# One attention unit of a decoder trunk, laid out anew over all engine queues

## The chip, the cores and the metric

The kernel runs on one core of one Trainium2 chip. Its time is the device time of one execution, in microseconds (us). TensorE is called PE here and its weight loads PEld, VectorE is DVE, ScalarE is ACT, GpSimd is POOL, and SP is the engine whose queue issues most transfers. Each engine works through its own queue in program order, and waits there for what it needs from the others.

## The reference

The reference is one layer of a decoder trunk over 2048 positions of width 1024. One wide product gives queries, keys, values, gates and the input of a pooling branch; a sliding-window attention with sinks and a multi-scale causal pool are mixed through gates, projected, and normalised. What matters here is the attention: 16 query heads share 2 key heads, and each block of 128 queries sees 256 keys.

```python
logits = jnp.einsum('bnqhgd,bnkhd->bnhgqk', qb, kb) * (HEAD_DIM ** -0.5) + bias
logits = jnp.where(mask[None, :, None, None], logits, NEG_INF)
probs = jax.nn.softmax(jnp.concatenate([logits, sink], axis=-1), axis=-1)[..., :-1]
out = jnp.einsum('bnhgqk,bnkhd->bnqhgd', probs.astype(v.dtype), vb)
...
a = sliding_window_sink_attention(q, k, v, sinks[l], bias, mask) * jax.nn.silu(a_gate)
p = jnp.einsum('bsgc,gcd->bsgd', multiscale_causal_pool(p_in), w_pool_mix[l]).reshape(B, S, POOL_WIDTH)
```

## The kernel before

The kernel goes through five stages: gate products, attention over the first 1024 positions, gate products again, attention over the second 1024, and the projections with the normalisation. A product in full precision is made of rounded high parts and the rests (low parts): a function `low` subtracts the rounded high part from a number, and three matmuls replace one.

The function `attention` runs once for each half. It has 64 units, numbered `n`; a unit is two heads of one block of 128 queries. Its loop makes five turns more than that, in which the last units drain. A unit passes through a pipeline that spans several turns of the loop:

- PE makes its scores, `lg` (`score_mms`, four matmuls of 256 columns).
- For each of the two heads, DVE adds the bias to the scores and takes the running minimum of the negated sum (`tensor_tensor_reduce`, which the profile calls CUSTOM_DVE_ANT_0; writes `L` and `nm`), and ACT makes the exponentials of it in place, with their sum (`sm`).
- DVE takes the reciprocal of the two sums. ACT scales head 0 with it and DVE scales head 1 (`tensor_scalar`).
- PE turns the probabilities (`turn_mms`, into the bank `pt`), ACT rounds them to `pth`, and DVE makes the low part `ptl` from `pt` and `pth`.
- PE multiplies both with the values (`value_mms`, into the bank `pv`). High and low halves of the values lie in two halves of the partitions, so ACT copies one half to `o2`, and DVE adds it to the other, into `o` (two additions).

The buffers `pt`, `pv`, `pth` and `ptl` exist once, `lg` twice, `L` three times. Beside this, each turn of the loop holds a piece of other work: `project(n)` issues 9 or 12 matmuls of 512 columns from another product, which give later queries and the pooling input (`fill_one` issues 12 matmuls of the next stage in the last turns). When such a product ends, its result is taken at the end of a turn: `take_q` makes two ACT casts and two DVE operations that form new queries `qs`; `pool_sums` and `pool_diff` do the pooling on ACT, POOL and DVE (`vb`, `nxt`). Splitting weights into parts (`w_set`) uses ACT, and POOL or DVE.

No scheduler reorders these: the helper class `Ordered` keeps an engine's instructions in the order in which the Python code issues them, so all of them carry line 56 of that helper in the profile. The order of the statements in the loop is thus the order in each queue.

Of the kernel before, what the change touches and what calls it, by code (L numbers as in the profile page):

```python
# [59 lines left out]
def kernel(  # L60
# [675 lines left out]
    def attention(ph, s, q0, nxt):  # L736
# [149 lines left out]
        bts = {0: bias_tile(0)}  # L886
        raw_q = {}
        parts, accs, sums = {}, {}, {}
        lgs, exps, Ls, pvs, outs, ags, pgs = {}, {}, {}, {}, {}, {}, {}
        opened = []  # L890
        act.activation(warm, mhalf, AF.Exp)

# [32 lines left out]
        for n in range(N + 5):  # L925
# [1 line left out]
            if n == 0:  # L927
                project(n)
            if n < N:
                lgs[n] = score_mms(j, n % U, b, qs[j, t])  # L930
            pt = None
            if n - 2 in Ls:
                L, k0 = Ls.pop(n - 2)
                pt = turn_mms(L, k0)
            if n - 1 in exps:
                sm = exps[n - 1][2]
                dve.reciprocal(sm, sm)
            if n - 3 in pvs:
                pv = pvs.pop(n - 3)
# [5 lines left out]
                o2 = tp.tile([HD, 2, P], F32, tag="o2", bufs=2, name="o2")  # L945
                act.copy(o2, pv[HD:])
                for h in range(2):
                    dve.tensor_tensor(
                        outs[jj, tt][h * HD : (h + 1) * HD, bb * P : (bb + 1) * P], pv[0:HD, h, :], o2[:, h, :], ALU.add
                    )  # L950
            if n - 1 in exps:
                E, e0, sm = exps[n - 1]
                act.activation(E[:, 0, e0:256], E[:, 0, e0:256], AF.Copy, scale=sm[:, 0:1])
            if pt is not None:
                h0 = k0 // P
                pth = tp.tile([P, 2, 2, P], F32R, tag="pth", bufs=1, name="pth")
                ptl = tp.tile([P, 2, 2, P], F32R, tag="ptl", bufs=1, name="ptl")
                act.copy(pth[:, h0:], pt[:, h0:])
            if n < N:
                lg, c0 = lgs.pop(n)  # L960
                L = tp.tile([P, 2, 260], F32, tag="L", bufs=3, name="L")
                nm = tp.tile([P, 2], F32, tag="nm", bufs=4, name="nm")
                sm = tp.tile([P, 2], F32, tag="sm", bufs=4, name="sm")
                act.copy(L[:, :, 256], nsink[:, 2 * j : 2 * j + 2])
                for h in range(2):
                    dve.tensor_tensor_reduce(
                        L[:, h, c0:256],
                        lg[:, h, c0:],
                        bts[j][:, h, c0:],
                        1.0,  # L970
                        nsink[:, 2 * j + h : 2 * j + h + 1],
                        ALU.add,
                        ALU.min,
                        nm[:, h : h + 1],
                    )
                    act.activation(
                        L[:, h, c0:257],
                        L[:, h, c0:257],
                        AF.Exp,
                        bias=nm[:, h : h + 1],  # L980
                        scale=-1.0,
                        accum_out=sm[:, h : h + 1],
                    )
                exps[n] = (L, c0, sm)
# [10 lines left out]
            if pt is not None:  # L995
# [549 lines left out]
```

## Time and profile before

| | |
|---|---|
| median of 3 runs | 1771.92 us (1771.76 to 1773.22) |
| profiled execution | 1771.75 us, its span 1769.9 us, granted clock 0.992 |
| PE busy | 1701.8 us, 96% of the span |
| PEld busy | 1422.5 us, 80% |
| DVE, ACT, POOL busy | 68%, 53%, 45% |
| attention stages | about 424 to 690 us and 1030 to 1300 us from the start |

Busy time says how much of the span an engine had an instruction under way. The ends of matmuls are modelled in this profile and the rows overlap by some 0.15 us, so a PE row that follows at once begins before the modelled end of the one ahead. A row of the timeline gives start, length, engine, line, operation, written tile and read tiles, and in brackets how long the engine sat idle before it and what released it. Rows with "x4" are merged neighbours.

### The profile page before, as it was taken

Reading aid. Unit: us, or ns where it says so; the run is one execution under the profiler, and the core shown is the slowest. Engines: PE = TensorE matmul, PEld = TensorE weight load, DVE = VectorE, ACT = ScalarE, POOL = GpSimd, SP = SyncE. Lnnn points to the kernel's source line nnn. Section 1 sums busy time; section 2 is a strip of 40 time slices with the busy share of each in tenths; the row PEclk is TensorE's granted clock in tenths of the full one; section 3 lists DMA queues with packets and bytes.
Section 4 is the critical chain, followed back from the end, with each engine's and each line's share of the span. In section 5 each row is a group of like instructions: output and inputs, shape, how many; then the busy total and the mean of one; then the engine's idle time right before and its main releaser. Section 6 shows DMA issues by size and latency. Waiting matters only on the chain. (4 is left out here: it accounts for less than half of the span.)

```text
span 1769.9 us, 24992 instructions
## 1 busy us (share of the span) xinstructions
PE 1701.8 (96%) x8224; PEld 1422.5 (80%) x8224; DVE 1212.4 (68%) x2188; ACT 941.5 (53%) x1983; POOL 803.5 (45%) x624
## 2 busy tenths in 40 slices
PE   6899999999999998999999999999999989999997
PEld 5688888888888887888788888888878767888785
DVE  5977656546777777767745457777867676865777
ACT  4644444436777776444444367777744333423452
POOL 2155444530545567433424224455763663363542
PEclk9999999999999999999999999999999999999998
DMA  9385767853434467687776544454696684699432
GB/s 364 119 287 178 266 215 262 286 130 125 167 135 166 147 230 301 242 276 262 260 273 230 188 162 163 141 178 136 246 355 221 191 261 170 240 322 366 155 143 107
DMA packets 182161, 383.40 MB, mean 217 GB/s; under 512 B 18944, under 2 KB 39440, under 8 KB 182032
## 3 DMA queue, kind: packets, MB, share of 16 engines
q1 hardware_dynamic: 175392, 366.02, 59.1%
q0 software_dynamic: 3552, 11.56, 1.7%
q10 hardware_dynamic: 3088, 4.23, 0.9%
q8 instruction: 65, 1.06, 0.2%
q14 instruction: 64, 0.52, 0.1%
HBM read 245.40 MB, written 139.49 MB: 217 GB/s over the span
## 5 line engine op out<-in xcount | busy, mean ns | idle before, releaser
L56 PE MATMUL mm<-set_B,w_set 128*128 128x512 f32 x3096 | 768.5, 395 | 12.4 <-DVE w_set L133 5.5
L56 PEld LDWEIGHTS mm<-set_B,w_set 128*128 128x128 f32 x3096 | 577.3, 189 | 134.2 <-DVE w_set L133 10.6
L56 PE MATMUL lg<-set_T,w_set 128*128 128x512 f32 x2160 | 523.6, 392 | 17.3 <-DVE w_set L133 9.3
L56 PEld LDWEIGHTS lg<-set_T,w_set 128*128 128x128 f32 x2160 | 404.2, 188 | 110.8 <-DVE w_set L133 14.9
L133 DVE TENSOR_TENSOR w_set<-W,w_set 128x1024 fp32r<-128x1024 f32 x168 | 232.2, 1382 | 205.4 <-ACT w_set L326 195.2
L326 ACT CAST w_set<-W 128x1024 fp32r<-128x1024 f32 x168 | 176.3, 1050 | 266.8 <-PE mm L56 204.9
L56 PE MATMUL mm<-set_T,w_set 128*128 128x512 f32 x1032 | 257.6, 394 | 0.0
L56 PEld LDWEIGHTS mm<-set_T,w_set 128*128 128x128 f32 x1032 | 192.3, 189 | 39.5
L295 POOL TENSOR_TENSOR W<-W,A 128x512 f32<-128x512 f32 x58 | 86.5, 1491 | 237.9 <-DMA A<-in_win_dram 58.2
L304 POOL TENSOR_TENSOR W<-W 128x512 f32<-128x512 f32 x58 | 81.8, 1410 | 189.0 <-DVE w_set L133 178.7
L56 ACT ACTIVATE L<-L,nm 128x257 f32<-128x257 f32 (+1 forms) x256 | 127.1, 498 | 11.0 <-DVE nm L56 5.7
L299 POOL TENSOR_TENSOR W<-W 128x512 f32<-128x512 f32 x58 | 92.0, 1587 | 89.5 <-DVE w_set L133 80.4
L56 DVE TENSOR_TENSOR o<-pv,o 64x128 f32<-64x128 f32 x256 | 72.4, 283 | 81.0 <-ACT o L56 77.9
L56 DVE CUSTOM_DVE_ANT_0 L<-lg,bt,nsink 128x256 f32<-128x256 f32 (+1 forms) x256 | 111.6, 473 | 5.7 <-PE lg L56 1.7
L300 POOL TENSOR_TENSOR W<-W 128x512 f32<-128x512 f32 x58 | 94.6, 1630 | 43.8 <-DMA W<-in_win_dram 27.6
L56 POOL TENSOR_TENSOR p<-nxt,pg 128x512 f32<-128x512 f32 x32 | 41.3, 1292 | 113.5 <-DVE sm L56 113.0
L56 POOL TENSOR_TENSOR nxt<-vb 128x512 f32<-128x512 f32 (+3 forms) x32 | 34.2, 1068 | 122.7 <-ACT vb L56 122.7
L56 DVE TENSOR_TENSOR ptl<-pt,pth 128x512 fp32r<-128x512 f32 (+1 forms) x128 | 85.6, 669 | 1.7 <-ACT pth L56 1.5
L56 ACT COPY o<-pv 64x256 f32<-64x256 f32 x128 | 47.3, 370 | 66.1 <-PE pv L56 65.0
L56 DVE TENSOR_TENSOR k_lo<-spare,k_hi 128x512 fp32r<-128x512 f32 x61 | 61.4, 1009 | 30.0 <-ACT k_hi L56 13.2
L56 ACT ACTIVATE L<-L,sm 128x256 f32<-128x256 f32 (+1 forms) x128 | 64.3, 502 | 31.6 <-DVE sm L56 31.6
L56 PE MATMUL lg<-kk,qs 128*128 128x256 f32 (+1 forms) x512 | 80.3, 279 | 0.0
(217 smaller groups left out, 2347.3 us busy)
## 6 DMA issues: line engine op xcount, KB each, us to landing
W<-in_win_dram SPq DMA_DIRECT2D x48, 512.0 KB, 4.9
w_set<-wmix_d SPq DMA_DIRECT2D x28, 512.0 KB, 4.7
W<-in_win_dram SPq DMA_DIRECT2D x36, 256.0 KB, 3.2
A<-in_win_dram SPq DMA_DIRECT2D x36, 256.0 KB, 4.5
ag_d<-sig SPq DMA_DIRECT2D x32, 256.0 KB, 3.5
pg_d<-sig SPq DMA_DIRECT2D x32, 256.0 KB, 3.5
ma_d<-sig SPq DMA_DIRECT2D x32, 256.0 KB, 4.0
mp_d<-sig SPq DMA_DIRECT2D x32, 256.0 KB, 3.7
```

The costliest lines, as they stand in the source:

```text
L56: return lambda *args, **kw: self.tc.keep_in_program_order(op(*args, **kw))
L133: engine.tensor_tensor(dst, src, as32(hi), ALU.subtract)
L295: e.tensor_tensor(self.w[:, 1, :], self.w[:, 2, :], self.a22, ALU.add)
L299: e.tensor_tensor(x[:, 1, :], x[:, 1, :], x[:, 0, :], ALU.subtract)
L300: e.tensor_tensor(x[:, 2, :], x[:, 0, :], x[:, 2, :], ALU.subtract)
L304: e.tensor_tensor(x[:, 3, :], x[:, 3, :], x[:, 1, :], ALU.subtract)
L326: a.copy(by_two(hi), raw)
```

## The change

Nothing is computed differently, and no instruction is added or removed. The statements in the loop of `attention` stand in another order:

- the value products of a unit are issued one turn later, behind the next unit's scores and ahead of the turning of the unit between;
- the other work of the turn (`project` or `fill_one`) is issued straight after the PE work of the attention;
- ACT copies the sink column and scales head 0 ahead of the copy `o2` and the rounding to `pth`;
- the minimum and the exponentials are made for head 1 first, then head 0;
- on DVE the two additions into `o` come behind the two minima, ahead of the low part `ptl`;
- the reciprocal and the scaling of head 1 come at the end of the unit's own turn, behind its exponentials, and no longer in the next turn.

```diff
             if n < N:
-                lgs[n] = score_mms(j, n % U, b, qs[j, t])
-            pt = None
+                lg, c0 = score_mms(j, n % U, b, qs[j, t])
+            pt = pv = None
+            if n - 3 in turned:
+                pv = value_mms((n - 3) // U, (n - 3) % U, *turned.pop(n - 3))
             if n - 2 in Ls:
                 L, k0 = Ls.pop(n - 2)
-                pt = turn_mms(L, k0)
-            if n - 1 in exps:
-                sm = exps[n - 1][2]
-                dve.reciprocal(sm, sm)
-            if n - 3 in pvs:
...
+                pt, h0 = turn_mms(L, k0), k0 // P
+            if 0 < n < 60:
+                project(n)
+            elif n >= 60:
+                fill_one(n)
...
+                act.copy(L[:, :, 256], nsink[:, 2 * j : 2 * j + 2])
             if n - 1 in exps:
-                E, e0, sm = exps[n - 1]
-                act.activation(E[:, 0, e0:256], E[:, 0, e0:256], AF.Copy, scale=sm[:, 0:1])
+                E, e0, r = exps.pop(n - 1)
+                act.activation(E[:, 0, e0:256], E[:, 0, e0:256], AF.Copy, scale=r[:, 0:1])
+                Ls[n - 1] = (E, e0)
+            if pv is not None:
+                o2 = tp.tile([HD, 2, P], F32, tag="o2", bufs=2, name="o2")
+                act.copy(o2, pv[HD:])
             if pt is not None:
...
                 act.copy(pth[:, h0:], pt[:, h0:])
-                for h in range(2):
+            for h in (1, 0) if n < N else ():
                     dve.tensor_tensor_reduce(
...
+            if pv is not None:
...
                 for h in range(2):
                     dve.tensor_tensor(
                         outs[jj, tt][h * HD : (h + 1) * HD, bb * P : (bb + 1) * P], pv[0:HD, h, :], o2[:, h, :], ALU.add
                     )
             if pt is not None:
                 low(dve, ptl[:, h0:], pt[:, h0:], pth[:, h0:])
-            if n - 1 in exps:
-                E, e0, sm = exps.pop(n - 1)
-                dve.tensor_scalar(E[:, 1, e0:256], E[:, 1, e0:256], sm[:, 1:2], None, ALU.mult)
-                Ls[n - 1] = (E, e0)
-            if 0 < n < 60:
-                project(n)
-            elif n >= 60:
-                fill_one(n)
-            if pt is not None:
-                pvs[n - 2] = value_mms((n - 2) // U, (n - 2) % U, k0, pth, ptl)
+                turned[n - 2] = k0, pth, ptl
+            if n < N:
+                dve.reciprocal(sm, sm)
+                dve.tensor_scalar(L[:, 1, c0:256], L[:, 1, c0:256], sm[:, 1:2], None, ALU.mult)
+                exps[n] = (L, c0, sm)
```

How the queues stand is shown at one place, in the first attention: the turn whose end takes new queries, and the turn behind it. In these lists `mm<-set,w_set` are the matmuls of `project`, `pv` the value products, `lg` the scores, and `pt` the turning. First PE, before:

```order
L56 MATMUL mm<-set_B_68,w_set 128x512 x3
L56 MATMUL mm<-set_T_237,w_set 128x512 x6
L56 MATMUL pv<-pth,vv 128x256
L56 MATMUL pv<-ptl,vv 128x256
L56 MATMUL pv<-pth,vv 128x256
L56 MATMUL pv<-ptl,vv 128x256
L56 MATMUL lg<-kk,qs 128x256 x4
L56 MATMUL pt<-ident,L 128x128 x4
L56 MATMUL mm<-set_T_237,w_set 128x512 x6
```

and PE at the same place after the change:

```order
L56 MATMUL mm<-set_B_68,w_set 128x512 x3
L56 MATMUL mm<-set_T_237,w_set 128x512 x6
L56 MATMUL lg<-kk,qs 128x256 x4
L56 MATMUL pv<-pth,vv 128x256
L56 MATMUL pv<-ptl,vv 128x256
L56 MATMUL pv<-pth,vv 128x256
L56 MATMUL pv<-ptl,vv 128x256
L56 MATMUL pt<-ident,L 128x128 x4
L56 MATMUL mm<-set_T_237,w_set 128x512 x6
```

The four score matmuls of the next unit now stand between the other work and the value products; everything else on PE keeps its place.

DVE at the same place, before. `ISA L,nm` is a minimum and `ISA nm` the reading of its result; `TENSOR_SCALAR` is the scaling of head 1, and `qs` the new queries:

```order
L56 TENSOR_TENSOR ptl<-pt,pth 128x512
L56 TENSOR_SCALAR L<-L,sm 128x256
L56 SCALAR_TENSOR_TENSOR qs<-mm,qs 64x512 x2
L56 RECIPROCAL sm<-sm 128x2
L56 TENSOR_TENSOR o<-pv,o_4152 64x128 x2
L56 ISA L,nm<-lg,bt,nsink 128x256
L56 ISA nm 128x1
L56 ISA L,nm<-lg,bt,nsink 128x256
L56 ISA nm 128x1
L56 TENSOR_TENSOR ptl<-pt,pth 128x512
L56 TENSOR_SCALAR L<-L,sm 128x256
```

and DVE after:

```order
L56 TENSOR_TENSOR ptl<-pt,pth 128x512
L56 RECIPROCAL sm<-sm 128x2
L56 TENSOR_SCALAR L<-L,sm 128x256
L56 SCALAR_TENSOR_TENSOR qs<-mm,qs 64x512 x2
L56 ISA L,nm<-lg,bt,nsink 128x256
L56 ISA nm 128x1
L56 ISA L,nm<-lg,bt,nsink 128x256
L56 ISA nm 128x1
L56 TENSOR_TENSOR o<-pv,o_4168 64x128 x2
L56 TENSOR_TENSOR ptl<-pt,pth 128x512
L56 RECIPROCAL sm<-sm 128x2
L56 TENSOR_SCALAR L<-L,sm 128x256
```

The reciprocal went from behind the new queries to ahead of them, and the additions from ahead of the minima to behind them; the scaling now belongs to the turn's own unit.

ACT at the same place, before (`L,sm<-L,nm x2` are the two exponentials, `L<-L,sm` the scaling of head 0):

```order
L56 ACTIVATE L,sm<-L,nm 128x257 x2
L56 CAST w_set<-W 128x1024
L56 ACTIVATE qs<-mm 64x512 x2
L56 COPY o_4152<-pv 64x256
L56 ACTIVATE L<-L,sm 128x256
L56 CAST pth<-pt 128x512
L56 COPY L<-nsink 128x2
L56 ACTIVATE L,sm<-L,nm 128x257 x2
```

and ACT after:

```order
L56 ACTIVATE L,sm<-L,nm 128x257 x2
L56 CAST w_set<-W 128x1024
L56 ACTIVATE qs<-mm 64x512 x2
L56 COPY L<-nsink 128x2
L56 ACTIVATE L<-L,sm 128x256
L56 COPY o_4168<-pv 64x256
L56 CAST pth<-pt 128x512
L56 ACTIVATE L,sm<-L,nm 128x257 x2
```

The sink copy and the scaling moved ahead of the copy `o2`. POOL's queue and SP's hold the same work in the same order, but for a few stores into device memory that pass one neighbour.

More of the change, by code (lines that the diff above doesn't have):

```diff
@@ L938, in attention @@
-            if n - 3 in pvs:
-                pv = pvs.pop(n - 3)
+                pt, h0 = turn_mms(L, k0), k0 // P
[4 more added lines that the diff above has]
+            if n < N:
+                L = tp.tile([P, 2, 260], F32, tag="L", bufs=3, name="L")
+                nm = tp.tile([P, 2], F32, tag="nm", bufs=4, name="nm")
+                sm = tp.tile([P, 2], F32, tag="sm", bufs=4, name="sm")
+                act.copy(L[:, :, 256], nsink[:, 2 * j : 2 * j + 2])
@@ new lines, in attention @@
+            if n - 1 in exps:
+                E, e0, r = exps.pop(n - 1)
[4 more added lines that the diff above has]
+                act.copy(o2, pv[HD:])
+            if pt is not None:
+                pth = tp.tile([P, 2, 2, P], F32R, tag="pth", bufs=1, name="pth")
+                ptl = tp.tile([P, 2, 2, P], F32R, tag="ptl", bufs=1, name="ptl")
+                act.copy(pth[:, h0:], pt[:, h0:])
@@ new lines, in attention @@
+            for h in (1, 0) if n < N else ():
+                dve.tensor_tensor_reduce(
+                    L[:, h, c0:256],
+                    lg[:, h, c0:],
+                    bts[j][:, h, c0:],
+                    1.0,
+                    nsink[:, 2 * j + h : 2 * j + h + 1],
+                    ALU.add,
+                    ALU.min,
+                    nm[:, h : h + 1],
+                )
+                act.activation(
+                    L[:, h, c0:257],
+                    L[:, h, c0:257],
+                    AF.Exp,
+                    bias=nm[:, h : h + 1],
+                    scale=-1.0,
+                    accum_out=sm[:, h : h + 1],
+                )
@@ L944, in attention @@
                     ags[jj, tt] = ld("ag", gates_d["ag"][s, jj, tt])
-                o2 = tp.tile([HD, 2, P], F32, tag="o2", bufs=2, name="o2")
-                act.copy(o2, pv[HD:])
                 for h in range(2):
@@ L950, in attention @@
                     )
-            if n - 1 in exps:
-                E, e0, sm = exps[n - 1]
-                act.activation(E[:, 0, e0:256], E[:, 0, e0:256], AF.Copy, scale=sm[:, 0:1])
-            if pt is not None:
[L955 to L964, printed above, removed]
-                for h in range(2):
[L966 to L984, printed above, removed]
```

4 lines of the change are left out of this document (2 added, 2 removed).

## The prediction

> **What bounds the kernel now.** I read the busy time by stage first, since only the two attention stages are touched. The columns after the name of the stretch are its length and the busy time of PE, PEld, DVE, ACT and POOL:
>
> ```profile
> 424.00:690.00 266.00, 261.29 (x1483) 225.20 (x1482) 203.05 (x630) 203.58 (x607) 148.27 (x122) 1.00 0.50 175
> 1030.00:1300.00 270.00, 264.83 (x1515) 229.33 (x1514) 206.83 (x630) 206.31 (x605) 148.47 (x116) 1.00 0.50 175
> ```
>
> PE is the bound in both: it is busy for 98%, while DVE has 266.00 - 203.05 = 62.95 us to spare over 64 units, 0.98 us a unit. PE's work stays the same, so the change can give only what PE waits. Next I read the waits of the weight loads and of the matmuls, for the first and the second stretch (us in total, times, longest):
>
> ```profile
> PEld pv L56 <- DVE ptl L56: 6.7, 11, 0.7
> PEld pv L56 <- ACT pth L56: 2.6, 5, 0.9
> PE pv L56 <- DVE ptl L56: 3.7, 9, 0.6
> PE pv L56 <- ACT pth L56: 0.7, 2, 0.5
> ...
> PEld pv L56 <- DVE ptl L56: 7.4, 11, 0.7
> PEld pv L56 <- ACT pth L56: 2.2, 4, 0.9
> PE pv L56 <- DVE ptl L56: 4.3, 10, 0.5
> PE pv L56 <- ACT pth L56: 0.7, 2, 0.5
> ```
>
> Almost every wait is that of a value product for its operands. The loads give 6.7 + 2.6 + 7.4 + 2.2 = 18.9 us, the matmuls only 3.7 + 0.7 + 4.3 + 0.7 = 9.4. To choose between the two I take the dearest stall and count starts:
>
> ```profile
> 480.24 0.95 PE L56 MATMUL mm<-set_B,w_set 128*128 128x512 f32 x3
> 481.02 1.55 PE L56 MATMUL mm<-set_T,w_set 128*128 128x512 f32 x6
> 483.08 0.38 PE L56 MATMUL pv<-pth,vv 128*128 128x256 f32 x1 [0.51 <-ACT pth L56]
> 484.02 0.38 PE L56 MATMUL pv<-ptl,vv 128*128 128x256 f32 x1 [0.55 <-DVE ptl L56]
> 484.48 0.64 PE L56 MATMUL lg<-kk,qs 128*128 128x256 f32 x4
> 484.95 0.27 PE L56 MATMUL pt<-ident,L 128*128 128x128 f32 x1
> ...
> 480.24 0.37 ACT L56 COPY o<-pv 64x256 f32<-64x256 f32 x1
> 481.91 0.51 ACT L56 ACTIVATE L<-L,sm 128x256 f32<-128x256 f32 x1 [1.30 <-DVE sm L56]
> 482.45 0.59 ACT L56 CAST pth<-pt 128x512 fp32r<-128x512 f32 x1
> 482.93 0.20 ACT L56 COPY L<-nsink 128x2 f32<-128x2 f32 x1
> ...
> 480.25 1.39 DVE L56 SCALAR_TENSOR_TENSOR qs<-mm,qs 64x512 fp32r<-64x512 f32 x2 [2.01 <-ACT qs L56]
> 481.65 0.17 DVE L56 RECIPROCAL sm<-sm 128x2 f32<-128x2 f32 x1
> 481.85 0.58 DVE L56 TENSOR_TENSOR o<-pv,o 64x128 f32<-64x128 f32 x2
> 482.46 0.48 DVE L56 CUSTOM_DVE_ANT_0 L<-lg,bt,nsink 128x256 f32<-128x256 f32 x1
> 482.87 0.48 DVE L56 CUSTOM_DVE_ANT_0 L<-lg,bt,nsink 128x256 f32<-128x256 f32 x1
> 483.28 0.68 DVE L56 TENSOR_TENSOR ptl<-pt,pth 128x512 fp32r<-128x512 f32 x1
> ```
>
> and beside it a unit without a stall:
>
> ```profile
> 565.43 2.31 PE L56 MATMUL mm<-set_B,w_set 128*128 128x512 f32 x9
> 567.59 0.28 PE L56 MATMUL pv<-pth,vv 128*128 128x256 f32 x1
> 567.71 0.29 PE L56 MATMUL pv<-ptl,vv 128*128 128x256 f32 x1
> 566.43 0.51 ACT L56 ACTIVATE L<-L,nm 128x257 f32<-128x257 f32 x1
> 567.34 0.18 ACT L56 ACTIVATION_READ_ACCUMULATOR L<-L,nm 128x1 f32 x1
> 566.63 0.69 DVE L56 TENSOR_TENSOR ptl<-pt,pth 128x512 fp32r<-128x512 f32 x1
> ```
>
> Without a stall a value product starts 565.43 + 2.31 - 567.59 = 0.15 us before the modelled end of the project matmuls, and the low-part product 0.12 later. At the stall that would be 481.02 + 1.55 - 0.15 = 482.42 and 482.54; it was 484.02, so 1.48 us were lost. The two matmul rows show 0.51 + 0.55 = 1.06 of them. So I go by the loads: 18.9 us, in 11 + 11 = 22 stalls, is all that can be won. The Trainium skill ("Perfetto Trace Analysis", Identifying the Most-Contended Engine) says that matmul busy time is no good measure of headroom, because pipelined matmuls look different in the trace than they are, and that load busy time serves better. The trace agrees by the starts just counted (1.48 against 1.06); by matmul idle alone the whole prize would be 9.4 us and the time no lower than 1762.3.
>
> The cause stands in the same rows. New queries keep DVE until 481.64. Behind them wait the reciprocal, for which ACT waits 1.30 us with the scaling and behind it with `pth`, and the additions and both minima, behind which the low part `ptl` waits. In the quiet unit `ptl` ends at 567.32 and is used at 567.71: 0.39 us of slack, so any piece of DVE work beyond that becomes a stall.
>
> **The change, part by part.** Instructions are the same in number and kind on every engine, so all terms are waits.
>
> Scores ahead of the value products: the scores need nothing from the late chain (`lg` has two banks and their queries are older), so PE does them inside the wait. From 484.48 to 484.95 they take 0.47 us. Each stall loses up to that, and the work is not added elsewhere.
>
> Reciprocal and scaling ahead of the new queries: the chain to `ptl` loses the reciprocal, 481.65 to 481.85, 0.20 us. The new place of both lies in the time in which DVE waits 2.01 us for the casts of the new queries. The waits for `pth` go altogether: ACT would do the scaling straight after the casts and the sink copy, so `pth` would end well before 482.42.
>
> Additions behind the minima: between the new queries and `ptl` both stand in either order, so at a stall this is worth nothing. In a quiet unit the minima now fill the time before `o2`; I cost that at nothing, since no stall is there to be shortened.
>
> At the shown stall: queries end at 481.64, two minima 2 x 0.41, additions 0.61, low part 0.68 and 0.06 until PE has it, which is 483.82; PE would be ready for it at 482.54 + 0.47 = 483.01. 0.81 us remain of 1.48: 0.67 saved, 0.47 + 0.20.
>
> The new wait is that of the reciprocal for the second exponential, with the scaling, `take_q` and `pool_diff` queued behind it on DVE, and ACT's next scaling waiting for it. From the start of the first exponential to the end of the last sum pass 567.52 - 566.43 = 1.09 us. The exponentials follow `pth` directly (next start 0.48 after it, 482.45 to 482.93), so they end 1.57 after `pth` began; the low part begins at 0.63 and lets DVE go at 1.23 (0.60 each). The reciprocal waits some 0.35 us, where DVE is on time; where DVE is late, the minima and so the low part are late too and the exponentials end behind them. From below the wait is 0, from above 1.09 (all of the exponentials exposed); I take 0.35, as the nearest rows give it. It lies within DVE's 0.98 of spare time, and what waits for it is needed one turn later: price 0. Without that cover it would push the new queries back and eat the 0.20.
>
> Value products a turn later keep `pv`, `pth` and `ptl` one score longer, 0.47 us. Their next writers come behind the same products in PE's order or after turning, so nothing new waits. `o2`, and POOL's product of `o` with the gate, come about 0.5 us later; a whole turn of POOL work covers that. The few stores that pass a neighbour on SP's queue read finished tiles and feed later stages: price 0.
>
> The sum: 22 x 0.67 = 14.7 us, less what the small stalls do not have. These are the ones below 0.67:
>
> ```profile
> 462.38 0.19 PEld L56 LDWEIGHTS pv<-ptl,vv 128*128 128x128 f32 x1 [0.44 <-DVE ptl L56]
> 519.92 0.19 PEld L56 LDWEIGHTS pv<-ptl,vv 128*128 128x128 f32 x1 [0.40 <-DVE ptl L56]
> 620.76 0.19 PEld L56 LDWEIGHTS pv<-ptl,vv 128*128 128x128 f32 x1 [0.54 <-DVE ptl L56]
> 656.04 0.19 PEld L56 LDWEIGHTS pv<-ptl,vv 128*128 128x128 f32 x1 [0.51 <-DVE ptl L56]
> 1066.17 0.19 PEld L56 LDWEIGHTS pv<-ptl,vv 128*128 128x128 f32 x1 [0.61 <-DVE ptl L56]
> 1124.24 0.19 PEld L56 LDWEIGHTS pv<-ptl,vv 128*128 128x128 f32 x1 [0.39 <-DVE ptl L56]
> ```
>
> They lack 0.23 + 0.27 + 0.13 + 0.16 + 0.06 + 0.28 = 1.13 us. 14.7 - 1.1 = 13.6 us are saved. The profiled execution took 1771.75 us, 0.17 below the median of the runs: 1771.75 - 13.6 = 1758.2. What is late next is `ptl` at the stalls with both waits, by the remaining 0.1 to 0.8 us.
>
> **The rivals.** *Only the scores count.* If the reciprocal's wait pushes the new queries back by as much as it shortened the chain, 0.47 us remain for each stall: 22 x 0.47 less 0.2 for the three smallest is 10.1 us, 1761.6. For it speaks that some scalings last long (below), against it the 2.01 us of waiting.
>
> *All stalls go.* The exponentials start without the sink copy ahead of them and the minima come earlier, so ACT's casts and the new queries could start some 0.2 us earlier, and the chains that remain could shrink to nothing: 1771.75 - 18.9 = 1752.9. Against it: the shown stall would need 0.8 us more.
>
> *Nothing comes of it.* If DVE's work between two new queries, and not its order, sets when `ptl` is ready, PE waits for the same work at another place, and the time stays at 1771.9. Against it speaks DVE's idle time, 2.01 us in the very turn that stalls.
>
> *Slower: the scaling of head 1 meets POOL behind the new wait.* Its length varies:
>
> ```profile
> L56 DVE TENSOR_SCALAR L<-L,sm x64: 275/346/1468, 430.6 to 683.9; 128x256 f32<-128x256 f32 x56, 128x128 f32<-128x128 f32 x8
> L56 DVE TENSOR_SCALAR L<-L,sm 128x256 f32<-128x256 f32 (+1 forms) x64 | 34.3, 536 | 0.0
> ```
>
> 346 ns at the median, 1468 at the most, 536 in the mean. If at its new place each took the longest, a unit would gain 0.93 us and the wait of 0.35, 1.28 against 0.98 to spare: DVE would become the bound by 0.30 us a unit, 128 x 0.30 = 38 us over a PE without stalls, 1752.9 + 38 = 1791. It decides from about 0.98 us of added DVE time a unit. Against it: POOL is busy for 148.27 of 266 us, so most would still meet it idle, as now. The Trainium skill ("SBUF — State Buffer", Who interferes with whom) explains such a spread: a `tensor_scalar` may enter a mode that takes the port pair shared with GpSimd, and whichever starts second is blocked for the whole of the other's instruction. The spread of the row fits that; by the rule the mean goes with POOL's share, which the change leaves alone, and the sum stays.
>
> **How the numbers follow.** A difference of 0.2% (3.5 us) is about what a measurement of this kernel tells from none. Forecast (1756 to 1760) 0.46; only the scores, or a little less (1760 to 1765) 0.22; all or nearly all stalls gone (1752.9 to 1756) 0.13; nothing, within 0.2%, 0.10; slower 0.07; a gain between 3.5 and 7 us 0.02. Range 1752.9 to 1765, with 0.81 inside. Faster 0.83, same 0.10, slower 0.07.
>
> **What would show it.** Right: the value products' waits in the loads fall from 18.9 to about 5 us, none of them for `pth`; ACT's wait for `sm` goes; DVE waits before the reciprocal for ACT, some 0.2 to 0.4 us in many units; both stretches shorten by 6 to 7 us each, all others stay. Wrong: waits of the scores for DVE's minima, or of DVE for the reciprocal above 0.9 us a unit with scalings near 1.4 us; or loads that still wait 0.5 us and more after every set of new queries.

## The result, and the profile after

| | before | after |
|---|---|---|
| median (range, runs) | 1772.57 us (1771.76 to 1774.95, 4) | 1759.05 us (1756.23 to 1761.95, 4) |
| ratio, 95% interval | | 0.9922 [0.9902, 0.9942] |
| profiled execution, granted clock | 1771.75 us, 0.992 | 1761.95 us, 0.990 |

The kernel became 13.5 us faster; 1758.2 was predicted. The execution that was profiled is the longest of the four: from the last turning of its second attention to its end it takes 482.04 us, where the kernel before takes 477.85 and the other twelve kernels of this document 473.6 to 478.2. So the stages are compared, and not the whole. The length of an attention is read from the timeline, from ACT's first sink copy to the start of PE's last turning. After the change (start, length, engine, operation):

```profile
429.70 0.18 ACT L56 COPY L<-nsink 128x2 f32<-128x2 f32 x1
679.08 0.60 PE L56 MATMUL pt<-ident,L 128*128 128x128 f32 x4
...
1024.34 0.18 ACT L56 COPY L<-nsink 128x2 f32<-128x2 f32 x1
1278.16 0.60 PE L56 MATMUL pt<-ident,L 128*128 128x128 f32 x4
```

That is 249.38 and 253.82 us. The same four rows of the kernel before start at 427.50, 685.00, 1030.58 and 1292.05, which makes 257.50 and 261.47. Both attentions are shorter, by 8.1 and 7.7 us, 15.8 together. Such a length repeats well: two kernels below that share this loop but for one detail (the order of the heads in one, the place of one load in the other) have 503.18 and 503.53 us for both attentions, against 503.20 here. The waits of the value products' loads over the whole trace, after (us in total, times, longest):

```profile
PEld pv L56 <- DVE ptl L56: 2.3, 7, 0.5
```

Before, this wait was 14.1 us and the one for `pth` 4.8, 18.9 together; the one for `pth` is gone. The place that the prediction had worked out, the turn that takes new queries near 480 us, after:

```profile
481.21 1.54 PE L56 MATMUL mm<-set_T,w_set 128*128 128x512 f32 x6
482.59 0.63 PE L56 MATMUL lg<-kk,qs 128*128 128x256 f32 x4
483.18 0.36 PE L56 MATMUL pv<-pth,vv 128*128 128x256 f32 x1
483.81 0.39 PE L56 MATMUL pv<-ptl,vv 128*128 128x256 f32 x1 [0.27 <-DVE ptl L56]
...
480.22 1.39 DVE L56 SCALAR_TENSOR_TENSOR qs<-mm,qs 64x512 fp32r<-64x512 f32 x2 [1.48 <-ACT qs L56]
481.64 0.49 DVE L56 CUSTOM_DVE_ANT_0 L<-lg,bt,nsink 128x256 f32<-128x256 f32 x1
482.05 0.49 DVE L56 CUSTOM_DVE_ANT_0 L<-lg,bt,nsink 128x256 f32<-128x256 f32 x1
482.45 0.57 DVE L56 TENSOR_TENSOR o<-pv,o 64x128 f32<-64x128 f32 x2
483.06 0.69 DVE L56 TENSOR_TENSOR ptl<-pt,pth 128x512 fp32r<-128x512 f32 x1
483.67 0.16 DVE L56 RECIPROCAL sm<-sm 128x2 f32<-128x2 f32 x1
```

The scores stand inside the former stall, DVE goes from the queries to the minima without the reciprocal, and the product of the low part starts at 483.81. The prediction had 483.82 (its terms add up to 483.81). The new queries start at almost the same time in both profiles, 480.25 and 480.22, so the chain from them to `ptl` can be compared directly: 3.57 us were forecast and 3.59 measured.

One thing came back elsewhere. At the end of the first attention PE waits longer for the next stage's first operand:

```profile
692.23 10.20 PE L56 MATMUL mm<-set_B,w_set 128*128 128x512 f32 x36 [6.51 <-ACT u L377]
```

Before, this wait was 4.67 us, at 696.27, so it grew by 1.8 us. Whether this costs the kernel 1.8 us is open: from the last turning of the first attention to the first sink copy of the second pass 345.26 us after the change and 345.58 before, no more than before.

### The profile page after: what moved, and what is told of

It is laid out like the page before. It is cut to its first block, busy times and chain, and to the rows that moved or that the text cites. A ratio compares the mean times of both kernels' runs of the same rounds, so it can differ in the third digit from the quotient of the medians.

```text
span 1760.2 us, 24851 instructions
## 1 busy us (share of the span) xinstructions
PE 1698.5 (96%) x8224; PEld 1424.7 (81%) x8224; DVE 1227.9 (70%) x2188; ACT 934.3 (53%) x1983; POOL 804.4 (46%) x624
## 5 line engine op out<-in xcount | busy, mean ns | idle before, releaser
L304 POOL TENSOR_TENSOR W<-W 128x512 f32<-128x512 f32 x58 | 83.5, 1442 | 182.2 <-DVE w_set L133 174.7
L299 POOL TENSOR_TENSOR W<-W 128x512 f32<-128x512 f32 x58 | 90.1, 1554 | 99.7 <-DVE w_set L133 90.7
L56 ACT ACTIVATE L<-L,nm 128x257 f32<-128x257 f32 (+1 forms) x256 | 126.9, 500 | 12.0 <-DVE nm L56 11.8
L300 POOL TENSOR_TENSOR W<-W 128x512 f32<-128x512 f32 x58 | 90.0, 1552 | 43.5 <-DMA W<-in_win_dram 28.7
L56 PEld LDWEIGHTS lg<-kk,qs 128*128 128x128 f32 x512 | 77.9, 189 | 9.9
L56 ACT CAST pth<-pt 128x512 fp32r<-128x512 f32 (+1 forms) x128 | 73.4, 573 | 7.3
```

The costliest lines, as they stand in the source:

```text
L56: return lambda *args, **kw: self.tc.keep_in_program_order(op(*args, **kw))
L299: e.tensor_tensor(x[:, 1, :], x[:, 1, :], x[:, 0, :], ALU.subtract)
L300: e.tensor_tensor(x[:, 2, :], x[:, 0, :], x[:, 2, :], ALU.subtract)
L304: e.tensor_tensor(x[:, 3, :], x[:, 3, :], x[:, 1, :], ALU.subtract)
```

## The experiments

Theory A is the prediction's sum: each edit has a price of its own, 0.47 us a stall for the scores, 0.20 for the reciprocal, nothing for the additions and for ACT's order. The first four kernels do one part of the change alone.

**The value products alone** (pe_only):

```diff
+            if n - 3 in turned:
+                pvs[n - 3] = value_mms((n - 3) // U, (n - 3) % U, *turned.pop(n - 3))
...
-                pvs[n - 2] = value_mms((n - 2) // U, (n - 2) % U, k0, pth, ptl)
+                turned[n - 2] = k0, pth, ptl
```

> The kernel before with one part of the change: the value products go behind the next unit's scores on PE, all else stands as before. Theory A (each of the 22 stalls loses what stands in front of the waiting product: one group of scores, 0.47 us): the value products' waits in the weight loads fall from 18.9 to about 8.8 us, the time by 10 us, to 1762. Rival B (the scores only move the wait, PE waits as long at the same product): waits near 18.9, time 1772. Rival C (the copy o2 and the additions come 0.47 us later, and with them the minima and the low part, so nothing is won): waits near 18, with the low part later by 0.47 in quiet turns, time 1771.

1774.45 us against 1772.98, ratio 1.001 [0.9999, 1.0021]: nothing, nearest to rival C. The turn that stalls and the one ahead of it show why (PE, ACT, DVE):

```profile
476.14 0.64 PE L56 MATMUL lg<-kk,qs 128*128 128x256 f32 x4
476.61 0.28 PE L56 MATMUL pv<-pth,vv 128*128 128x256 f32 x1
...
485.83 0.38 PE L56 MATMUL pv<-ptl,vv 128*128 128x256 f32 x1 [0.54 <-DVE ptl L56]
...
477.29 0.37 ACT L56 COPY o<-pv 64x256 f32<-64x256 f32 x1 [1.44 <-PE pv L56]
477.56 0.51 ACT L56 ACTIVATE L<-L,sm 128x256 f32<-128x256 f32 x1
478.10 0.59 ACT L56 CAST pth<-pt 128x512 fp32r<-128x512 f32 x1
478.89 0.51 ACT L56 ACTIVATE L<-L,nm 128x257 f32<-128x257 f32 x1
...
482.06 1.39 DVE L56 SCALAR_TENSOR_TENSOR qs<-mm,qs 64x512 fp32r<-64x512 f32 x2 [1.99 <-ACT qs L56]
```

ACT waits 1.44 us for `pv`, and behind that wait stand, in its queue, the scaling, `pth`, both exponentials and the casts of the new queries. Counted from where PE begins this piece of its queue (first score or value product of the turn), the queries start on DVE after 482.06 - 476.14 = 5.92 us; in the kernel before it was 480.25 - 474.76 = 5.49. So the queries come 0.43 us later, about what the scores save inside the stall (0.47). The stall stays as long as it was: PE's next scores start at 483.75, so it would be ready for the low-part product at 483.75 + 0.47 + 0.12 = 484.34 and gets it at 485.83, 1.49 us later; before it was 1.48.

**The reciprocal alone** (recip_only): the reciprocal and head 1's scaling go to the end of their own turn.

```diff
+            if n < N:
+                dve.reciprocal(sm, sm)
+                dve.tensor_scalar(L[:, 1, c0:256], L[:, 1, c0:256], sm[:, 1:2], None, ALU.mult)
+                exps[n] = (L, c0, sm)
```

> The kernel before with one part of the change: reciprocal and scaling of head 1 at the end of the unit's own turn, ahead of the new queries. Theory A: the chain to the low part gets shorter by the reciprocal, 0.20 us a stall; waits for pth in the loads vanish, but the low part still sets the end: waits fall from 18.9 to about 14.5 us, time 1767.5. Rival (the wait for pth was the real cause): waits fall by the 4.8 us of pth and more, to below 12, time 1763 or less. Rival (the reciprocal's new wait for the exponentials costs): waits at 18.9 or more, DVE waits for ACT before the reciprocal by more than 0.5 us a turn, time 1772 or more.

1775.24 us, ratio 1.0016 [1.0006, 1.0025]. The wait for `pth` goes, as foretold; the stalls for `ptl` get longer (whole trace):

```profile
PEld pv L56 <- DVE ptl L56: 17.4, 24, 1.3
```

DVE's wait for `o2` falls (`DVE o <- ACT o`, 77.9 us before, 43.7 here, over the trace), but DVE now waits for the exponentials as well (`DVE sm <- ACT L`, 4.0 before, 32.5 here), and ACT's exponentials for the minima (`ACT L <- DVE nm`, 5.7 before, 38.0 here). The additions still stand ahead of the minima; that they are what hands ACT's lateness on is read from the order of the queues and not varied in this kernel.

**The additions alone** (adds_only):

```diff
-                for h in range(2):
-                    dve.tensor_tensor(
...
+                add = jj, tt, bb, pv, o2
...
+            if add is not None:
+                jj, tt, bb, pv, o2 = add
+                for h in range(2):
+                    dve.tensor_tensor(
...
             if pt is not None:
                 low(dve, ptl[:, h0:], pt[:, h0:], pth[:, h0:])
```

> The kernel before with one part of the change: the additions behind the two minima on DVE. Theory A: at a stall both stand ahead of the low part in either order, nothing is won there: waits 18 to 19 us, time 1771 to 1772. Rival (in quiet turns DVE waits for o2 in front of the additions, 78 us in all; filled with the minima, the exponentials and all that follows start earlier and the stalls shrink): waits below 14 us, time 1767 or less.

1775.4 us, ratio 1.0014 [1.0004, 1.0023]. DVE no longer waits for `o2` ahead of the additions; it waits as long for the scores ahead of the minima instead (`DVE L <- PE lg`, 77.9 us over the trace, where the wait for `o2` was 77.9 before). The loads wait about as much as before (18.0 us for 18.9), in part for another reason (whole trace):

```profile
PEld pv L56 <- DVE ptl L56: 9.6, 20, 0.5
PEld pv L56 <- ACT L L56: 8.1, 16, 1.2
```

The bank `pv` exists once, and the next value product has to wait until the additions, now later, have read it. The loads put this down to `ACT L`; the matmuls' own rows name the additions in part:

```profile
PE pv L56 <- DVE o L56: 2.1, 5, 0.8
```

The prediction had held that no writer of these banks would have to wait. The attentions are 1.1 us shorter than before, but PE's wait at the first one's end is 6.35 us, as after the whole change, and not 4.67.

**ACT's order alone** (act_only): the sink copy and head 0's scaling ahead of `o2`.

```diff
+            if n < N:
...
+                act.copy(L[:, :, 256], nsink[:, 2 * j : 2 * j + 2])
+            if n - 1 in exps:
+                E, e0, sm = exps[n - 1]
+                act.activation(E[:, 0, e0:256], E[:, 0, e0:256], AF.Copy, scale=sm[:, 0:1])
             if n - 3 in pvs:
                 pv = pvs.pop(n - 3)
```

> The kernel before with one part of the change: ACT's order alone (sink copy and scaling of head 0 ahead of the copy o2). Theory A: the scaling waits for a reciprocal that still stands behind the new queries on DVE, and o2 now waits behind the scaling; the additions wait for o2 and the low part for the additions: some 0.9 us more at each of the 22 stalls and 0.1 to 0.5 us in quiet turns, so slower, 1785 to 1800, waits 35 us or more. Rival (the order on ACT is hidden): waits 18.9, time 1772.

1822.67 us, ratio 1.0282 [1.0267, 1.0298]: 50 us slower.

```profile
PEld pv L56 <- DVE ptl L56: 47.3, 52, 1.3
PEld pv L56 <- ACT pth L56: 15.6, 20, 2.1
```

In the old order the reciprocal stands behind the new queries, so ACT waits for it with `o2` behind (`ACT L <- DVE sm`, 70.1 us), DVE's additions wait for `o2` (`DVE o <- ACT o`, 137.9 us), and the minima stand behind these.

Four parts, and none of them a gain in time: theory A has fallen. Theory A2, formed here: the queues form a loop. PE's value products release ACT's `o2`; behind it in ACT's queue stand the exponentials and the casts; those release DVE's new queries; behind these stand the minima, additions and `ptl`, which release the value products. An edit gains only if no other queue puts the time back into the loop. The next four kernels, and a fifth, leave one part out of the change. Each is the changed kernel with the named statement back at its old place.

**Without the value products' move** (no_pe):

```diff
-            if n - 3 in turned:
-                pv = value_mms((n - 3) // U, (n - 3) % U, *turned.pop(n - 3))
+            if n - 3 in pvs:
+                pv = pvs.pop(n - 3)
...
-                turned[n - 2] = k0, pth, ptl
+                pvs[n - 2] = value_mms((n - 2) // U, (n - 2) % U, k0, pth, ptl)
```

> The kernel after with one part undone: the value products stand ahead of the next unit's scores again. The first runs refuted theory A: scores alone gave nothing, since the copy o2 comes 0.47 us later with them, and behind it on ACT the scaling, pth, the exponentials and the casts of the new queries. Theory A2: ACT's chain is the one that counts; with scaling and sink copy ahead of o2 it starts at the turning either way, so here the exponentials come some 0.2 us earlier than before and the chain to the low part is 0.2 us shorter: 0.4 of some 0.85 us a stall, waits about 10 us, time 1766. Rival B2 (the scores are what matters once the rest is in place): waits above 14 us, time 1769 to 1772. Rival (PE's order is worth nothing even here): waits 2 to 4 us, time 1759.

1763.65 us, ratio 0.995 [0.9935, 0.9965]. The loads wait 11.2 us, where A2 had about 10, and the time is 2 us below its 1766.

**Without the reciprocal's move** (no_recip):

```diff
-                E, e0, r = exps.pop(n - 1)
+                E, e0, r = exps[n - 1]
+                dve.reciprocal(r, r)
...
+            if n - 1 in exps:
+                E, e0, r = exps.pop(n - 1)
+                dve.tensor_scalar(E[:, 1, e0:256], E[:, 1, e0:256], r[:, 1:2], None, ALU.mult)
+                Ls[n - 1] = (E, e0)
...
-                dve.reciprocal(sm, sm)
-                dve.tensor_scalar(L[:, 1, c0:256], L[:, 1, c0:256], sm[:, 1:2], None, ALU.mult)
```

> The kernel after with one part undone: reciprocal and scaling of head 1 one turn later, as before, behind the new queries. Theory A2: the scaling of head 0 on ACT waits for that reciprocal again, and o2 and pth stand behind it; pth ends some 0.5 us later than in the kernel after and the low part with it: waits 10 to 15 us, time 1766 to 1770. Rival (only the reciprocal's own 0.2 us counts): waits 5 to 7 us, time 1763. Rival (its new wait for the exponentials costs something, so that undoing it helps): time below 1758.

1765.31 us, ratio 0.9959 [0.9943, 0.9975]. ACT again waits for `sm` (76.3 us over the trace, 11.2 in the changed kernel), and the loads for 5.1 + 1.7 us, of which 1.7 for `pth`. The direction is A2's, the size is not: it had waits of 10 to 15 us, and 6.8 came, inside the 5 to 7 of the first rival.

**Without the additions' move** (no_adds): the block moves as a whole.

```diff
+            if pv is not None:
+                jj, tt, bb = (n - 3) // U, (n - 3) // NB % 2, (n - 3) % NB
...
             for h in (1, 0) if n < N else ():
...
-            if pv is not None:
-                jj, tt, bb = (n - 3) // U, (n - 3) // NB % 2, (n - 3) % NB
```

> The kernel after with one part undone: the additions ahead of the minima. My prediction costed their place at nothing. Theory A2: with the value products behind the scores, o2 comes about 0.5 us later than before, and additions ahead of the minima would hand this on to the minima, the exponentials and the casts: 0.5 us a stall and less slack in quiet turns, waits 12 to 18 us, time 1768 to 1773. Rival (worth nothing): waits 2 to 4 us, time 1759.

1777.81 us, ratio 1.0034 [1.0013, 1.0054]: slower than the kernel before, by more than A2 had expected. The rows that carry it, first attention:

```profile
PEld pv L56 <- DVE ptl L56: 10.7, 15, 1.3
...
DVE o L56 <- ACT o L56: 27.4, 33, 1.5
DVE sm L56 <- ACT L L56: 15.5, 57, 0.8
...
ACT L L56 <- DVE nm L56: 49.3, 63, 2.0
```

With scores and scaling ahead of it, `o2` comes late; the additions wait for it at the head of DVE's queue, and the minima behind them, and ACT's exponentials wait for the minima in nearly every unit (97.3 us over the trace, 11.8 in the changed kernel).

**Without the change of heads** (no_heads):

```diff
-            for h in (1, 0) if n < N else ():
+            for h in (0, 1) if n < N else ():
```

> The kernel after with one part undone: head 0 first, then head 1. Theory A2: the two heads have the same sizes and the reciprocal waits for both, so nothing changes: waits 2 to 3 us, time 1757 to 1761. Rival (the order of the heads lets the scaling of head 1 start earlier): waits above 5 us, time 1763.

1756.31 us, ratio 0.9914 [0.9898, 0.9931], waits 2.2 us: the order of the two heads is worth nothing here.

**Without ACT's order** (no_act):

```diff
+                act.copy(o2, pv[HD:])
             if n - 1 in exps:
                 E, e0, r = exps.pop(n - 1)
                 act.activation(E[:, 0, e0:256], E[:, 0, e0:256], AF.Copy, scale=r[:, 0:1])
...
-                act.copy(o2, pv[HD:])
...
                 act.copy(pth[:, h0:], pt[:, h0:])
+            if n < N:
+                act.copy(L[:, :, 256], nsink[:, 2 * j : 2 * j + 2])
```

> The changed kernel with ACT's old order alone: the copy o2 first, then the scaling of head 0, pth, and the sink copy last. Theory A (the prediction: ACT's order is worth nothing by itself): as the changed kernel, 1757 to 1761 us, value products' loads waiting 2 to 3 us. Theory A2 (the chain through ACT sets when new queries are made): ACT waits for pv ahead of o2 in most turns, and the scaling and the sink copy, 0.4 + 0.1 us, now stand behind that wait, so first exponential, casts and new queries come some 0.45 us later; 22 x 0.45 = 10 us of waits come back, loads wait about 12 us, 1767 to 1770 us.

1769.91 us, ratio 0.9985 [0.9975, 0.9996]: as A2 had it, and 11 us above the changed kernel, where A had no difference. The loads wait 8.2 + 3.0 = 11.2 us (12 expected). The same turn, ACT and DVE:

```profile
477.24 0.37 ACT L56 COPY o<-pv 64x256 f32<-64x256 f32 x1 [1.52 <-PE pv L56]
477.51 0.51 ACT L56 ACTIVATE L<-L,sm 128x256 f32<-128x256 f32 x1
...
478.52 0.20 ACT L56 COPY L<-nsink 128x2 f32<-128x2 f32 x1
478.75 0.51 ACT L56 ACTIVATE L<-L,nm 128x257 f32<-128x257 f32 x1
...
481.92 1.39 DVE L56 SCALAR_TENSOR_TENSOR qs<-mm,qs 64x512 fp32r<-64x512 f32 x2 [1.48 <-ACT qs L56]
```

and of the changed kernel:

```profile
474.99 0.64 PE L56 MATMUL lg<-kk,qs 128*128 128x256 f32 x4
...
476.13 0.37 ACT L56 COPY o<-pv 64x256 f32<-64x256 f32 x1 [1.17 <-PE pv L56]
...
477.06 0.52 ACT L56 ACTIVATE L<-L,nm 128x257 f32<-128x257 f32 x1
```

From `o2` to the first exponential it is 478.75 - 477.24 = 1.51 us without ACT's order and 477.06 - 476.13 = 0.93 with it: the scaling and the sink copy are done in the time in which ACT would wait for `pv`. That 0.58 us reaches DVE whole (0.61). The queries start 481.92 - 476.08 = 5.84 us after the turn's scores (which start at 476.08 there), against 480.22 - 474.99 = 5.23. One more row of this kernel shows the bank named above; the engine waits for the additions, not for an operand:

```profile
484.88 0.35 PE L56 MATMUL pv<-pth,vv 128*128 128x256 f32 x1 [0.55 <-DVE o L56]
```

**Two parts together** (pe_adds): the kernel before with the edits of pe_only and adds_only.

> The kernel before with two parts of the change: value products behind the next scores, and additions behind the minima. Theory A: 0.47 us at each of 22 stalls, loads wait 9 to 10 us, 1762 to 1764 us. Theory A2: the additions behind the minima take away what held pe_only back (o2 being 0.5 us later), but ACT's scaling still stands behind o2 and in front of pth and the exponentials, and the reciprocal behind the new queries: loads wait 14 to 18 us, 1767 to 1771 us.

1772.92 us, ratio 1.0004 [0.9992, 1.0017]: still nothing, slightly above A2's range. The waits of the value products fell to 8.8 + 3.3 = 12.1 us, below A2's 14 to 18, but turnings now wait too, 3.4 us (0.6 before), and PE's wait at the first attention's end rose to 6.33 us.

All kernels side by side. The lengths of both attentions are added, read as above; the last column is the wait of the value products' loads over the whole trace, in us. The kernel before, measured again beside each group of kernels, had medians of 1771.7 to 1773.0 us:

| kernel | time | attentions | loads wait |
|---|---|---|---|
| before | 1772.57 | 518.97 | 18.9 |
| value products alone | 1774.45 | 520.38 | 14.7 |
| reciprocal alone | 1775.24 | 519.24 | 17.4 |
| additions alone | 1775.4 | 517.85 | 18.0 |
| ACT's order alone | 1822.67 | 570.80 | 62.9 |
| value products and additions | 1772.92 | 516.84 | 12.1 |
| all but the additions | 1777.81 | 526.35 | 20.5 |
| all but ACT's order | 1769.91 | 515.90 | 11.2 |
| all but the reciprocal | 1765.31 | 510.26 | 6.8 |
| all but the value products | 1763.65 | 511.29 | 11.2 |
| all but the heads | 1756.31 | 503.18 | 2.2 |
| after | 1759.05 | 503.20 | 2.3 |

A2 foretold that the additions and ACT's order, for which theory A had nothing, cost time when they are left out, and that parts bring little alone. Its sizes held only without ACT's order, and nearly without the change of heads and without the value products. It says which queues hand time on; the sizes it gives for that are not to be relied on.

**How much room is left in the loop** (after_low2):

```diff
+                for again in range(2):
-                low(dve, ptl[:, h0:], pt[:, h0:], pth[:, h0:])
+                    low(dve, ptl[:, h0:], pt[:, h0:], pth[:, h0:])
```

> The changed kernel with the low part ptl made twice in each unit (same result): 0.60 us more on DVE in the chain to ptl. Theory A2 (a serial chain through DVE and ACT, with 0.2 to 0.6 us still missing at the turns that take new queries and about 0.97 us to spare in others): 22 x 0.6 + 2.3 = 15 us of waits in the loads, 1770 to 1773 us. Rival (DVE's total work is what counts: 216 + 64 x 0.60 = 254 of some 262 us a stretch): waits in nearly every unit, 0.3 us or more each, loads wait over 40 us, above 1790 us.

1798.07 us, ratio 1.0145 [1.0124, 1.0167]. The attentions are 548.27 us long, 45 more than after the change, 0.35 a unit. A2 had 11 to 14 us more, counting on 0.97 us to spare in the turns without new queries; that was wrong, and the rival's time was right. The rival's waits were not: 36.7 us for "over 40", and in 42 loads of value products, not in nearly every unit. The busy times of both attentions together (length, then PE, PEld, DVE, ACT, POOL, then the means):

```profile
sum 548.27, PE 516.79 PEld 445.39 DVE 507.80 ACT 395.71 POOL 292.33; mean PE 258.40 PEld 222.70 DVE 253.90 ACT 197.85 POOL 146.17
```

DVE is busy for 93% of the attentions; in the changed kernel it was 413.02 of 503.20 us, 82%, or 0.70 us idle a unit. Its busy time grew by 0.74 us a unit and not by 0.60, since the scaling of head 1 got longer too (see the end of the next section). Of these 0.74 us only 0.39 found room. Which of DVE's idle time can be used, and which lies where it has to wait for another queue anyway, was not settled; that the turns without new queries have room for the whole of the added work is refuted.

**The loss at the end** (pg_early): the last load of the pooling gate two turns earlier.

```diff
-                if n == at + 2:
+                if n == at + 2 * (x != slots[-1]):
                     pgs[m, st] = ld("pg", gates_d["pg"][s, m, st])
```

> The changed kernel with the last load of the pooling gate (pg) of each attention issued two turns earlier, ahead of the loads of the next stage's sets. Theory G (what the change gives back at the attention's end comes from this load, which POOL's product p awaits for 2.58 us, against 0.51 before): POOL's wait goes, W behind it comes 1.0 to 2.6 us earlier, PE's wait for ACT's u at the end of the first attention falls from 6.5 to about 4.7 us; 1.5 to 2 us less than the changed kernel, 1757 us. Rival (W then waits for DVE's w_set, which is as late): PE still waits 6 us or more, time unchanged.

1755.58 us (1753.8 to 1757.36, 5 runs), ratio 0.9905 [0.9888, 0.9923]. POOL's rows after the change, then of this kernel:

```profile
674.47 2.29 POOL L56 TENSOR_TENSOR p<-nxt,pg 128x512 f32<-128x512 f32 x1 [2.58 <-DMA pg<-pg_d]
681.97 3.54 POOL L304 TENSOR_TENSOR W<-W 128x512 f32<-128x512 f32 x2
```

```profile
671.56 1.27 POOL L56 TENSOR_TENSOR p<-nxt,pg 128x512 f32<-128x512 f32 x1
679.11 1.29 POOL L304 TENSOR_TENSOR W<-W 128x512 f32<-128x512 f32 x1
681.94 1.29 POOL L304 TENSOR_TENSOR W<-W 128x512 f32<-128x512 f32 x1 [1.54 <-DVE w_set L56]
...
689.96 10.82 PE L56 MATMUL mm<-set_B,w_set 128*128 128x512 f32 x36 [4.63 <-ACT u L377]
```

POOL no longer waits for the load, its first `W` comes 2.9 us earlier (2.5 when counted from the start of the attention), and PE's wait falls from 6.51 to 4.63 us, back to what it was before the change. The second `W` then waits for DVE's `w_set`, which is the next thing late there. The median is 3.5 us below that of the changed kernel, but the intervals of the two kernels overlap, and where the difference arises is not settled. PE's wait at the first attention's end is 1.9 us shorter, yet the stretch from there to the second attention's first sink copy is not (346.38 us, 345.26 in the changed kernel). Behind the second attention PE waits less for a transfer of `set_T` (1.61 us before the change, 1.46 after it, 0.29 here). It is the fastest version that was run, beside the one without the change of heads.

Why the load came late is seen in SP's queue. Before the change, ahead of the load of `pg`:

```profile
658.78 0.36 SPq L56 DMA_DIRECT2D set_T<-u_T_split  x1
669.51 0.33 SPq L56 DMA_DIRECT2D ain_T<-a  x1
```

and after it:

```profile
663.78 0.33 SPq L56 DMA_DIRECT2D ain_T<-a  x1
664.21 0.94 SPq L56 DMA_DIRECT2D set_T<-u_T_split  x2
```

The store of `ain_T` has passed a neighbour, a load of `set_T`. This store waits for POOL (12.7 us here, 10.3 before), and the load, 1024 KB, which used to leave 10.7 us ahead of it, now leaves behind it together with the next one, directly ahead of `pg`. The load of `pg` (256 KB) takes 8.6 us from issue to landing, 7.0 before. All eight kernels with the additions behind the minima and `pg` at its old place have SP's queue in this new order, and POOL waits 2.3 to 3.1 us for `pg` in them; in the five with the additions ahead of the minima the old order stands, and it waits at most 0.6 us. So POOL's wait goes with the place of the additions. SP's order was not changed by itself, so that the order on SP makes the load late is argued from these rows.

## Why the prediction came out right, and where its steps did not

- *The total.* 13.6 us were forecast and 13.5 measured. That is partly luck: the attentions gained 15.8 us, more than forecast (8.1 and 7.7 against "6 to 7 each"), and 2.3 us of that are missing in the medians. PE's wait at the first attention's end, 1.8 us longer, may be a part of them; the prediction had nothing there ("all others stay").
- *The prize by the loads' waits.* 16.6 of 18.9 us went, and the attentions shortened by 15.8. By the matmuls' own idle time the whole prize would have been 9.4. The busy times of both attentions together, before and after, show what that misses:

```profile
sum 518.97, PE 509.10 PEld 440.17 DVE 396.69 ACT 399.25 POOL 288.81; mean PE 254.55 PEld 220.09 DVE 198.35 ACT 199.62 POOL 144.41
sum 503.20, PE 502.28 PEld 440.01 DVE 413.02 ACT 392.24 POOL 286.22; mean PE 251.14 PEld 220.01 DVE 206.51 ACT 196.12 POOL 143.11
```

  The same 2914 matmuls are shown as 6.8 us less busy, and the idle time of PE fell by 9.0; together these are the 15.8. The weight loads are as busy as before. The Trainium skill ("Perfetto Trace Analysis", Identifying the Most-Contended Engine) judges PE's headroom by load busy time and not by matmul busy time. The trace agrees that matmul busy time misleads; of waits of loads, by which the prediction went, the page says nothing. They overstate a single stall (0.95 + 0.74 = 1.69 us at the shown one, 1.48 by the starts) and the parts: without ACT's order the loads wait 7.7 us less than before and the attentions are only 3.1 shorter; with value products and additions 6.8 less, and 2.1 shorter, where PE's own idle time (length less busy time) fell by 1.9.
- *0.67 us a stall.* The stalls lost 16.6 / 22 = 0.75 us each, and the shown one 0.85 of its 1.48: PE was ready at 482.59 + 0.47 + 0.12 = 483.18, and got `ptl` at 483.81. But the split, 0.47 for the scores and 0.20 for the reciprocal, is refuted as prices that add up: each alone brought nothing. Left out they cost 4.6 and 6.3 us by the medians, 8.1 and 7.1 by the attentions' lengths, where the split has 10 and 4.
- *The step that failed* is "`o2`, and POOL's product of `o` with the gate, come about 0.5 us later; a whole turn of POOL work covers that". It followed `o2` to POOL only. `o2` is also at the head of ACT's queue, ahead of `pth`, the exponentials and the casts, and its reader is at the head of DVE's, ahead of the minima. That is where value products alone gave all of their gain away: the queries came 0.43 us later, and the stall kept its length (1.49 for 1.48).
- *Additions at nothing* was the term furthest off: left out, the kernel is 18.8 us slower than after the change, and slower than before. The sentence "between the new queries and `ptl` both stand in either order" is true of the turn that stalls, and misses the other turns, in which the additions wait for `o2` and hold the minima up.
- *The stores on SP's queue*, price 0, were a second such step: "the few stores that pass a neighbour on SP's queue" include `ain_T`. A load of 1024 KB now leaves behind it, directly ahead of the load of `pg`, for which POOL waits 2.58 us; with that load issued earlier, PE's 1.8 us of added wait at the first attention's end are gone.
- *ACT's order* had no term, and is worth 10.9 us in place, and minus 50 alone. The prediction used it only for the waits for `pth`, which went as foretold.
- *The reciprocal's new wait*, 0.35 us at price 0, held in size: 25.3 us in 80 waits over the trace, 0.32 each, the longest 0.8.

```profile
DVE L L56 <- PE lg L56: 30.5, 52, 1.4
DVE sm L56 <- ACT L L56: 25.3, 80, 0.8
```

  The row ahead of it is what now ends most of DVE's idle time in the attentions: it waits for PE's scores. Before, it waited most for `o2` there (77.9 us over the trace; after, 2.3).
- *The slower rival.* Head 1's scaling took this in the first attention after the change, against 275, 346 and 1468 ns before, 536 in the mean:

```profile
L56 DVE TENSOR_SCALAR L<-L,sm x64: 286/354/1625, 432.1 to 674.1; 128x256 f32<-128x256 f32 x56, 128x128 f32<-128x128 f32 x8
```

  Its mean is 573 ns (33.3 us in 56 and 3.4 in 8). In the second attention the mean went the other way, from 556 to 537 ns. So the rival did not come, and the sum needed no term for it. But the prediction's reason, that the mean goes with POOL's share, is not borne out: with the low part made twice the mean of the scalings of 128x256 is 707 and 723 ns (595 and 537 in the changed kernel), while POOL's busy share fell from 57% to 53%. What sets it was not tried.
- *ACT's wait for `sm`* was to go. It fell from 31.6 to 11.2 us.

## What to carry to other kernels

Where in-order queues hand work round in a loop, a move has to be followed through every queue whose instruction it makes later, and through all that stands behind that instruction, until the chain returns to the engine that is the bound. Parts of such a layout can't be priced by themselves: here four edits that each bring nothing or a loss in time give 13.5 us together, and to leave one out costs between 4.6 and 18.8. So try them together, take them out one at a time, and then look at the end of the stage, where a transfer that was just in time before has become late.

## What the runs showed that was not expected

A wait for a buffer can stand under a wrong name in the loads' rows: at the stall of no_act at 484.88, where `pv` was still being read by DVE's additions, the load names `ACT L` (0.73 us), and the matmul's own row names `DVE o` (0.55). And on SP's queue a store passed one load, and another load behind them came late: that of `pg`, issued at 665.70 us, let POOL go only at 674.47, 8.8 us later; issued two turns earlier, ahead of the store and of both loads of `set_T`, it made POOL wait no more.
